# A 23-column key block, raw output weights split inside attention, reordered first loads and a reordered end in a Trainium2 encoder layer

## The chip, the cores and the metric

The kernel runs on one core of one Trainium2 chip. Its engines are TensorE (PE: matmuls, and PEld for the loading of weights), VectorE (DVE), ScalarE (ACT), GpSimd (POOL) and SyncE (SP), whose queue issues nearly all transfers. Each engine takes its instructions in the order of its own queue. The time is that of one execution on the device, in microseconds; the span is the time from the first to the last instruction of the program in a profiled execution.

## The reference

An encoder layer runs over a prompt of 256 tokens and a sample of 2048 tokens, model width 1024, all in float32. After an RMS norm, one projection gives q, k, v, a gate z_a, u_f and a gate z_f, each 512 wide.

```python
q, k, v, z_a, u_f, z_f = jnp.split(proj, ...)
y_a = neighbourhood_attention(q, k, v, rpb)
y_f = fourier_mix(u_f, w_fourier, b_fourier)
mixed = jnp.concatenate([rms_norm(y_a, g_na) * jax.nn.silu(z_a),
                         rms_norm(y_f, g_f) * jax.nn.silu(z_f)], axis=-1)
out = mixed @ w_out
return x + rms_norm(out, g_post)
```

The tokens form a grid of 64 columns. In the neighbourhood attention, each of 8 heads (64 wide) lets a query see 8 rows and 16 columns of keys around it; the columns are worked in four blocks of 16 query columns, each against a slab of up to 32 key columns, with a table of biases added and everything outside the window masked. A query in column c sees key columns from clip(c-8, 0, 48) on, so the queries of the first block (columns 0 to 15) reach key column 22 at most: 23 columns. Fourier mixing is a two-dimensional FFT, a dense layer and a bias.

## The kernel before

Float32 matrices are split into a high and a low part in a reduced-precision type (`F32R`), and a product is made of three matmuls: high-high, high-low, low-high (`mm3`, lines 172 to 175). The stages, in order:

1. The v and u projections for the first row tiles. The first tile's inputs come in pieces (`x_part`, lines 623 to 650): a weight slice `RV`, the vector `gpre`, and x tiles 0, 1, 2. Nine matmuls on ones (`hot`) precede the first real one.
2. The other projections, in two halves of the channels' row groups (lines 749 to 963). Beside the second half, eight blocks of the output weights (128 rows by 1024) are loaded, scaled by `gmix`, split into high and low (`wo_load`, `wo_split`, lines 700 to 710) and stored in `woD`. Blocks 0 to 3 belong to the attention half of `mixed`, blocks 4 to 7 to the Fourier half.
3. The Fourier stage (lines 981 to 1347).
4. The attention stage, a loop over k (lines 1547 to 1635). There are 36 groups `G[k]`: four passes `pr` (two heads each), and in each pass one group for the prompt and eight for the sample, by row group R (0 to 3) and column half hc (0, 1). A group has two column blocks b, whose widths in key columns come from `KW` (line 31). In the loop, iteration k computes the scores of group k (`scores`), adds bias and takes the maximum on DVE (`bias_max`, L1193), exponentiates on ACT (`exps`, L1198), scales by the sum on POOL (`soft`, L1205); and of the group before it transposes the probabilities into the two tiles `ptb` (`transp`, L1469), copies them out (ACT L1471 for the first head, DVE L1473 for the second), and multiplies by V (`pv`, L1486). The PV result is gated on DVE (L1506), squared on ACT (L1512), and the squares are added on POOL (L1513). Between these PE does the Fourier half of the output projection (`f_mm`, L1415), six matmuls after each set of transposes. The order on PE, ACT, DVE, POOL and SP is that of the program text.
5. The attention half of the output projection (lines 1702 to 1733), and for the last tile `last_tile`.

In a group with R>0 a block of w key columns has 11 rows, so 11w keys for each head, in three chunks of 4w, 4w and 3w keys (`prep_v`, lines 1139 to 1142); with R=0 it has 8 rows in two chunks. The rows of the two query halves are laid so that the middle and last chunk hold the same keys for both halves, while the first differs between the halves; so the PV products are two of 128 columns for the shared chunks and two of 64 for the first, for each head.

The attention-half weights are read back from `woD` in iterations 24 to 31 (line 1564) into the two tiles `WO`, which the loop's last iteration (k=36) is the first to use. At the end, `last_tile` (lines 1679 to 1700) works in two column parts, and the residual of the tile before it is done inside it.

Of the kernel before, what the change touches and what calls it, by code (L numbers as in the profile page):

```python
# [18 lines left out]
T = TP + TS  # L19
# [11 lines left out]
KW = (24, 32, 32, 24)  # L31
# [13 lines left out]
def constants():  # L45
# [62 lines left out]
    for p in range(128):  # L108
        half, i, qc = p // 64, p // 16 % 4, p % 16
        for b in range(2):  # L110
            cb = 2 * b + half
            ws = min(max(16 * cb + qc - 8, 0), 48)
            kc = KP0[cb] + np.arange(32)
            cm[p, b] = np.where((kc >= ws) & (kc < ws + 16), 0.0, BIG)
        for cb, j in ((0, slice(0, 24)), (1, slice(24, 56)), (3, slice(56, 80))):
# [62 lines left out]
def build(tc, A, O):  # L178
# [20 lines left out]
    woD = dr.tile([2, 2, 4, 128, D], F32, name="woD")  # L199
# [169 lines left out]
    VC = ((0, 0, 0, 24, 0), (1, 0, 8, 24, 0), (1, 1, 0, 8, 24), (2, 0, 24, 8, 0), (2, 1, 0, 24, 8), (3, 1, 8, 24, 0))  # L369
# [266 lines left out]
    x_part(2, 0)  # L636
# [63 lines left out]
    def wo_load(x):  # L700
        wor[x] = load((128, D), A["wo"][x // 4, x % 4], "wr")

    def wo_split(x):
        w = wor.pop(x)
        g = gmix[:, x:x + 1]
# [3 lines left out]
        for y in range(2):  # L709
            nc.sync.dma_start(woD[x // 4, y, x % 4], f_(o[:, y]))  # L710
# [91 lines left out]
    def at(i, f, *a):  # L802
        hooks.setdefault(i, []).append(call(f, *a))
# [25 lines left out]
    for i in range(16):  # L829
        sg, pr = divmod(i, 8)  # L830
        if i == 8:
# [286 lines left out]
    def prep_v(g):  # L1118
# [99 lines left out]
    for n in range(2):  # L1218
        for c in range(4):
            nc.sync.dma_start(wo1[n][c].bitcast(F32),  # L1220
                              woD[1, :, c, :, n * 512:n * 512 + 512].rearrange("x p d -> p x d"))
# [301 lines left out]

    NT = {4: range(2, 4), 8: range(4, 8), 10: range(8, 13), 12: range(13, 18)}
# [22 lines left out]
    for k in range(2, len(G) + 1):  # L1547
# [11 lines left out]
        if k == 23:  # L1559
# [55 lines left out]
        if f:  # L1615
            pv(f)
        if k == 12:
            pq_.close()
# [40 lines left out]

    def factor(d, q=1):  # L1660
        sa, r = d["sa"], d["r"]
        s, y, x = r[:, 0:1], r[:, 1:2], r[:, 2:3]
        V.tensor_scalar(s, sa[:, q:q + 1], -0.5 / D, sa[:, 4:5], ALU.mult, ALU.add)
# [3 lines left out]
    def residual(d, n):  # L1667
        of, xt, s = d["of"], d["xt"], d["r"][:, 0:1]
        ns = slice(n * 512, n * 512 + 512)
        if "og" in d:  # L1670
            V.scalar_tensor_tensor(out=xt[:, ns], in0=d["og"][:, ns], scalar=s, in1=xt[:, ns], op0=ALU.mult,
                                   op1=ALU.add)
        else:
            V.scalar_tensor_tensor(out=of[:, ns], in0=ptb[n], scalar=s, in1=of[:, ns], op0=ALU.mult, op1=ALU.mult)
            nc.gpsimd.tensor_tensor(out=xt[:, ns], in0=of[:, ns], in1=xt[:, ns], op=ALU.add)
# [3 lines left out]
    def last_tile(d, b):  # L1679
# [12 lines left out]
        residual(b, 1)  # L1692
        sa = d["sa"]
        V.tensor_scalar(sa[:, 0:1], sa[:, 0:1], sa[:, 1:2], None, ALU.add)
# [55 lines left out]
```

## Time and profile before

| What | Value |
|---|---|
| Runs: lowest, median, highest | 959.3, 960.38, 962.52 us |
| The profiled execution | 960.57 us |
| Its span | 958.8 us |
| PE busy | 947.1 us (99%) |
| DVE, ACT, POOL busy | 670.5, 467.9, 332.5 us |
| Moved by DMA | 270.64 MB |
| Granted clock of PE | 0.998 |

In the profile, a row of a timeline gives the start and the length in microseconds, the engine, the line, the operation, what it writes and reads, the shape, and how many instructions were merged; in brackets stand the idle time before it and what ended it. A row of waits gives the total, the count and the longest one. A row of windows gives the stretch, then the busy time of PE, PEld, DVE, ACT and POOL, the granted clock and the share of the DMA engines. A row of one line gives the least, the median and the largest length in nanoseconds. In the timeline a `pv` or `s` product counts as two records.

### The profile page before, as it was taken

Reading aid. Unit: us, or ns where it says so; the run is one execution under the profiler, and the core shown is the slowest. Engines: PE = TensorE matmul, PEld = TensorE weight load, DVE = VectorE, ACT = ScalarE, POOL = GpSimd, SP = SyncE. Lnnn points to the kernel's source line nnn. Section 1 sums busy time; section 2 is a strip of 40 time slices with the busy share of each in tenths; the row PEclk is TensorE's granted clock in tenths of the full one; section 3 lists DMA queues with packets and bytes.
Section 4 is the critical chain, followed back from the end, with each engine's and each line's share of the span. In section 5 each row is a group of like instructions: output and inputs, shape, how many; then the busy total and the mean of one; then the engine's idle time right before and its main releaser. Section 6 shows DMA issues by size and latency. Waiting matters only on the chain.

```text
span 958.8 us, 17851 instructions
## 1 busy us (share of the span) xinstructions
PE 947.1 (99%) x6240; PEld 793.2 (83%) x6240; DVE 670.5 (70%) x1306; ACT 467.9 (49%) x1035; POOL 332.5 (35%) x335
## 2 busy tenths in 40 slices
PE   9999999999999999999999999999999999999996
PEld 7889988888888888888888888888887887888885
DVE  6387987677875975786767454676666555659997
ACT  6845677532333632233444144666565555544443
POOL 3100002445750300533433000454556555424444
PEclk9999999999999999999999999999999999999999
DMA  9899676468665998579979788589898899999993
GB/s 344 315 361 359 216 272 261 166 231 292 241 241 217 363 414 321 208 246 322 332 263 326 282 304 306 211 250 274 277 274 250 253 293 302 267 308 329 335 341 123
DMA packets 158361, 270.64 MB, mean 282 GB/s; under 512 B 22656, under 2 KB 98304, under 8 KB 155392
## 3 DMA queue, kind: packets, MB, share of 16 engines
q1 hardware_dynamic: 157984, 269.37, 81.4%
q8 instruction: 50, 0.82, 0.3%
q14 instruction: 39, 0.32, 0.1%
q10 hardware_dynamic: 288, 0.14, 0.1%
HBM read 180.91 MB, written 95.88 MB: 289 GB/s over the span
## 4 chain that ended last, share of the span: by engine, by line
PE 96%; DVE 1%; DMA 1%; issue 0%; ACT 0%; POOL 0%; DVEq 0%; ACTq 0%; POOLq 0%
PE po L1415 20%; PE mm L174 18%; PE mm L173 18%; PE mm L175 18%; PE pv L1486 5%; PE ptb L1469 5%; PE s L1171 4%; PE pab L1013 2%; PE py L173 1%; PE py L175 1%; PE py L174 1%; DMA yz<-zD 1%; DMA xr<-xt 0%; PE ppq L1051 0%; DMA q<-qD 0%
## 5 line engine op out<-in xcount | busy, mean ns | idle before, releaser
L173 PE MATMUL mm<-xh,wa 128*128 128x512 f32 x448 | 174.4, 389 | 0.0
L174 PE MATMUL mm<-xl,wa 128*128 128x512 f32 x448 | 174.3, 389 | 0.0
L175 PE MATMUL mm<-xh,wa 128*128 128x512 f32 x448 | 174.3, 389 | 0.0
L550 POOL TENSOR_TENSOR ws<-wr 128x512 f32<-128x512 f32 x16 | 21.4, 1336 | 262.4 <-DMA wr<-wz 256.4
L1205 POOL TENSOR_SCALAR w<-w,m 128x352 f32<-128x352 f32 (+4 forms) x136 | 76.9, 578 | 63.2 <-DVE m L1202 53.7
L175 PEld LDWEIGHTS mm<-xh,wa 128*128 128x128 f32 x448 | 84.1, 188 | 17.5
L173 PEld LDWEIGHTS mm<-xh,wa 128*128 128x128 f32 x448 | 84.1, 188 | 17.5
L174 PEld LDWEIGHTS mm<-xl,wa 128*128 128x128 f32 x448 | 84.1, 188 | 17.3
L1415 PE MATMUL po<-wo,yh 128*128 128x512 f32 x272 | 90.5, 413 | 0.0
L1415 PE MATMUL po<-w,yh 128*128 128x512 f32 x280 | 86.7, 391 | 0.0
L565 DVE TENSOR_TENSOR wa<-wr,wa 128x512 fp32r<-128x512 f32 x60 | 56.4, 946 | 30.9 <-ACT wa L564 30.8
L1198 ACT ACTIVATE w<-w,m 128x352 f32<-128x352 f32 (+4 forms) x136 | 70.3, 519 | 13.1 <-DVE m L1193 12.8
L867 DVE TENSOR_TENSOR f<-u,mm 128x512 f32<-128x512 f32 x64 | 43.5, 680 | 33.5 <-PE mm L175 28.7
L174 PE MATMUL mm<-vl,xh 128*128 128x512 f32 x168 | 65.5, 390 | 0.2 <-DVE vl L496 0.2
L175 PE MATMUL mm<-vh,xl 128*128 128x512 f32 x168 | 65.4, 389 | 0.0
L173 PE MATMUL mm<-vh,xh 128*128 128x512 f32 x168 | 65.4, 389 | 0.0
L1415 PEld LDWEIGHTS po<-w,yh 128*128 128x128 f32 x280 | 52.3, 188 | 10.7
L1193 DVE CUSTOM_DVE_ANT_1 w<-s,tb 128x264 f32<-128x264 f32 (+3 forms) x124 | 51.6, 453 | 11.1 <-PE s L1171 10.6
L564 ACT CAST wa<-wr 128x512 fp32r<-128x512 f32 x60 | 36.3, 617 | 41.5 <-PE mm L175 21.4
L1486 PEld LDWEIGHTS pv<-pt,v 96*64 96x64 f32 (+2 forms) x1088 | 45.0, 137 | 13.6 <-issue 9.6
L1415 PE MATMUL po<-w,yl 128*128 128x512 f32 x140 | 54.5, 389 | 0.0
L1415 PE MATMUL po<-wo,yl 128*128 128x512 f32 x136 | 53.5, 393 | 0.0
(244 smaller groups left out, 2204.9 us busy)
## 6 DMA issues: line engine op xcount, KB each, us to landing
wr<-wz SPq DMA_DIRECT2D x48, 512.0 KB
vl<-sD SPq DMA_DIRECT2D x20, 512.0 KB
xm<-xm SPq DMA_DIRECT2D x9, 1024.0 KB
oD<-ofs SPq DMA_DIRECT2D x18, 512.0 KB
of<-oD SPq DMA_DIRECT2D x18, 512.0 KB
yr<-yD SPq DMA_DIRECT2D x34, 256.0 KB
zD<-f SPq DMA_DIRECT2D x16, 512.0 KB
woD<-wo SPq DMA_DIRECT2D x16, 512.0 KB
```

The lines of the kernel that those rows point to most:

```text
L173: nc.tensor.matmul(out, lh, rh, start=first, stop=False)
L174: nc.tensor.matmul(out, lh, rl, start=False, stop=False)
L175: nc.tensor.matmul(out, ll, rh, start=False, stop=last)
L565: nc.vector.tensor_tensor(out=o[:, 1], in0=src, in1=o[:, 0].bitcast(F32), op=ALU.subtract)
L867: nc.vector.tensor_tensor(out=dst(f, b), in0=src(uu[u]), in1=src(p), op=op)
L1171: nc.tensor.matmul(sp[2 * b + h][64 * y:64 * y + 64, j * w:(j + n) * w], g["q"][hs, 128 * b + 64 * y:128 * b + 64 * y + 64], kk[hs, k:k + ...
L1193: nc.vector.tensor_tensor_reduce(out=rows(g["w"][b][:, h, :n], w), in0=rows(g["s"][2 * b + h][:, :n], w), in1=tv, scale=1.0, scalar=3.0e38 ...
L1198: nc.scalar.activation(w, w, AF.Exp, bias=m[:, h:h + 1], scale=-1.0, accum_out=m[:, 2 + h:3 + h])
L1205: nc.gpsimd.tensor_scalar(w, w, m[:, 4 + h:5 + h], 1.0, ALU.mult, ALU.mult)
L1415: nc.tensor.matmul(p, (d["l"] if x == 2 else d["h"])[:, c], w(n, int(x == 1), c), start=j == 0, stop=j == 11)
L1469: nc.tensor.transpose(ptb[h][:nk, j * 128:j * 128 + 128], g["w"][b][:, h, c0:c0 + nk], ident)
L1486: nc.tensor.matmul(p[hs, b, o], g["v"][:nk, v, hs], g["pt"][b][:nk, h, j * 128 + o.start:j * 128 + o.stop], start=first, stop=last)
```

## The change

The diff has four parts.

- The first column block has 23 key columns instead of 24 (`KW`, the masks, the copy of v). Where 11w is at most 256, `prep_v` makes two chunks, of 128 and 11w-128 keys, and loads V in three transfers instead of two.
- `wo_load` and `wo_split` treat the Fourier half only. The attention half is loaded raw within the attention loop, in eight pieces of 128 by 512 (odd k from 13 to 27) into a tile that takes a free slot, and each is split by one ACT and one DVE operation after `pv` in the even iterations from 18 to 32.
- The first requests: `gpre` and x tile 0 go to SP's queue, x tile 2 is the one request on ACT's queue.
- In `last_tile`, the sums come ahead of the residual of the tile before, one small operation comes ahead of a large one, and the last step is shared: 384 and 384 columns on DVE, 256 on ACT and POOL, in three transfers.

```diff
-KW = (24, 32, 32, 24)
+KW = (23, 32, 32, 24)
...
+    nc.sync.dma_start(gpre, A["gpre"])
+    x_part(2, 0, nc.scalar)
     nc.sync.dma_start(RV[0][:, 0], A["wv"][0][:, 0])
-    nc.scalar.dma_start(gpre, A["gpre"])
-    x_part(0, 0, nc.scalar)
+    x_part(0, 0)
...
     nc.sync.dma_start(RV[0][:, 1], A["wv"][0][:, 1])
     x_part(1, 0)
-    x_part(2, 0)
...
-            for x in range(8):
+            for x in range(4):
                 if x:
-                    at(3 * x - 2, wo_load, x)
-                at(3 * x + 2, wo_split, x)
+                    at(6 * x - 2, wo_load, x)
+                at(6 * x + 2, wo_split, x)
...
+            if g["R"] and 11 * w <= 256:
+                vs = src.rearrange("r c e -> (r c) e")[:, cs]
+                k0, k1, m = (r0 - 4) * w, (r1 + 3) * w, 11 * w - 128
+                nc.sync.dma_start(v[:, 4 * b:4 * b + 2], vs[k0:k0 + 256].rearrange("(j p) e -> p j e", p=128))
+                nc.sync.dma_start(v[:n, 4 * b + 2], vs[k1:k1 + n])
+                nc.sync.dma_start(v[n:, 4 * b + 2], vs[k0 + n:k0 + 128])
+                g["ch"].append([(0, 128), (128, m)])
+                g["pp"].append([(1, None, m, 4 * b + 1, True, False), (0, 0, 128, 4 * b, False, False),
+                                (0, 1, 128, 4 * b + 2, False, True)])
+                continue
...
+    def wo_split_a(y):
+        c, ns = wo_part(y)
+        h, l, w = WO[0][:, c, ns], WO[1][:, c, ns], wraw[:, y % 4 * 512:y % 4 * 512 + 512]
+        nc.scalar.activation(h, w, AF.Copy, scale=gmix[:, c:c + 1])
+        V.scalar_tensor_tensor(out=l, in0=w, scalar=gmix[:, c:c + 1], in1=h.bitcast(F32), op0=ALU.mult,
+                               op1=ALU.subtract)
...
-        if 24 <= k < 32:
-            y = k - 24
-            nc.sync.dma_start(WO[y % 2][:, y // 2].bitcast(F32), woD[0, y % 2, y // 2])
+        if 13 <= k < 29 and k % 2:
+            y = (k - 13) // 2
+            c, ns = wo_part(y)
+            nc.sync.dma_start(wraw[:, y % 4 * 512:y % 4 * 512 + 512], A["wo"][0, c][:, ns])
...
         if f:
             pv(f)
+        if 18 <= k < 34 and k % 2 == 0:
+            wo_split_a((k - 18) // 2)
...
-        residual(b, 1)
         sa = d["sa"]
         V.tensor_scalar(sa[:, 0:1], sa[:, 0:1], sa[:, 1:2], None, ALU.add)
         part_sum(sa)
+        residual(b, 1)
         guess(d, 3)
+        half_mean(d, 3)
         V.tensor_tensor(out=og[:, 512:], in0=ptb[1], in1=d["of"][:, 512:], op=ALU.mult)
         factor(d, 3)
-        for n in range(2):
-            residual(d, n)
+        xt, f = d["xt"], d["r"][:, 0:1]
+        nc.scalar.activation(og[:, 768:], og[:, 768:], AF.Copy, scale=f)
+        nc.gpsimd.tensor_tensor(out=xt[:, 768:], in0=og[:, 768:], in1=xt[:, 768:], op=ALU.add)
+        for q, ns in ((nc.sync, slice(0, 384)), (nc.sync, slice(384, 768)), (nc.scalar, slice(768, 1024))):
+            if ns.stop < D:
+                V.scalar_tensor_tensor(out=xt[:, ns], in0=og[:, ns], scalar=f, in1=xt[:, ns], op0=ALU.mult, op1=ALU.add)
+            q.dma_start(O["yo"][d["t"] * 128:d["t"] * 128 + 128, ns], xt[:, ns])
```

More of the change, by code (lines that the diff above doesn't have):

```diff
@@ L114, in constants @@
             cm[p, b] = np.where((kc >= ws) & (kc < ws + 16), 0.0, BIG)
-        for cb, j in ((0, slice(0, 24)), (1, slice(24, 56)), (3, slice(56, 80))):
+        for cb, j in ((0, slice(0, 23)), (1, slice(24, 56)), (3, slice(56, 80))):
             ws = min(max(16 * cb + qc - 8, 0), 48)
@@ L198, in build @@
     yD = dr.tile([2, 4, 128, T], F32, name="yD")
-    woD = dr.tile([2, 2, 4, 128, D], F32, name="woD")
+    woD = dr.tile([2, 4, 128, D], F32, name="woD")
     tD = dr.tile([4, 128, 2, 1520], F32, name="tD")
@@ L1522, in build, with wo_part @@
     WO = []
+    def wo_part(y):
+        return y // 2, slice(y % 2 * 512, y % 2 * 512 + 512)
+    def wo_split_a(y):
[4 more added lines that the diff above has]
+                               op1=ALU.subtract)
     NT = {4: range(2, 4), 8: range(4, 8), 10: range(8, 13), 12: range(13, 18)}
@@ L1669, in residual @@
         ns = slice(n * 512, n * 512 + 512)
[L1670 to L1675, printed above, removed]
+        V.scalar_tensor_tensor(out=of[:, ns], in0=ptb[n], scalar=s, in1=of[:, ns], op0=ALU.mult, op1=ALU.mult)
+        nc.gpsimd.tensor_tensor(out=xt[:, ns], in0=of[:, ns], in1=xt[:, ns], op=ALU.add)
         nc.sync.dma_start(O["yo"][d["t"] * 128:d["t"] * 128 + 128, ns], xt[:, ns])
```

20 lines of the change are left out of this document (12 added, 8 removed).

## The prediction

> **What bounds the kernel now.** I read the page first, then what TensorE (PE) waited for, then the timeline of the attention stage, the first ten microseconds and the last ten.
>
> ```profile
> span 958.8 us, 17851 instructions
> PE 947.1 (99%) x6240; PEld 793.2 (83%) x6240; DVE 670.5 (70%) x1306; ACT 467.9 (49%) x1035; POOL 332.5 (35%) x335
> ...
> PE 96%; DVE 1%; DMA 1%; issue 0%; ACT 0%; POOL 0%; DVEq 0%; ACTq 0%; POOLq 0%
> ```
>
> ```profile
> PE s L1171 <- DMA q<-qD: 0.9, 2, 0.5
> PE pv L1486 <- DMA v<-vD: 0.2, 1, 0.2
> ```
>
> ```profile
> 740.00:780.00 40.00, 40.00 (x477) 32.65 (x474) 23.90 (x85) 23.41 (x73) 21.91 (x35) 1.00 0.91 265
> ```
>
> PE is busy 947.1 of 958.8 us, and 96% of the chain is PE: the program is one long PE queue, idle for 11.7 us in all. In the attention stretch of the last row PE is busy 40.00 of 40.00 us, VectorE (DVE) 23.90, ScalarE (ACT) 23.41. So matmuls taken out of the queue pay in full, and work added to another engine costs nothing until it makes PE's next instruction late. The profiled execution took 960.57 us, 1.8 outside its span; the median of the runs is 960.38, 0.2 less.
>
> **23 columns.** The first column block belongs to groups with hc=0: one in each of four row groups R, in each of four passes pr. In the 12 with R>0, a head's keys shrink from 11x24=264 to 11x23=253, below 256, so three transposed chunks become two. Per group two transposes and two 128-column PV products (one per head) go; the two halves' 64-column products stay.
>
> ```profile
> 708.35 0.86 PE L1469 MATMUL ptb<-ident,w 128*96 128x128 f32 x6
> 746.12 0.66 PE L1469 MATMUL ptb<-ident,w 128*128 128x128 f32 x4
> 712.57 1.57 PE L1486 MATMUL pv<-pt,v 96*64 96x128 f32 x32
> 743.83 1.15 PE L1486 MATMUL pv<-pt,v 96*64 96x64 f32 x32
> 785.64 0.67 PE L1171 MATMUL s<-kk,q 64*64 64x128 f32 x16
> 791.97 0.99 PE L1171 MATMUL s<-kk,q 64*64 64x192 f32 x16
> ```
>
> Six transposes take 0.86, four 0.66: 0.2 for two, up to 0.22 with other pairs of rows. Two PV blocks of 32 records (16 products, two records each) differ only in that half of the products have 128 instead of 64 columns: 0.42 for 8 products, so 64 columns cost 0.0525; a 64-column product is 1.15/16=0.072, a 128-column one 0.125; two are 0.25. Score blocks of 128+128 and 192+256 columns differ by 0.32 over 192 columns, 1.7 ns a column: 11 fewer are 0.02. That is 12 x (0.21+0.25+0.02)=5.8, and about 0.1 for the four R=0 groups: **5.9 us off PE**. That chunks are now 128 keys deep costs nothing: the x6 row with 96-key weights is no shorter than those with 128. One more transfer per group for V lands at worst as late as the one wait on V above, 0.2 x 12=2.4; I take 0, since PE waited for V once in the whole stage, and that in the crowded stretch treated below.
>
> **The attention-half weights.** Before, eight 128x1024 blocks were split while the second half of the channels was projected; four of these splits, their four loads and eight stores go. No row of PE's waits names them, so taking them away gains 0; nor can it lose. In the attention stage eight stored blocks of 512 KB no longer come back; eight raw halves of 256 KB come earlier, in k=13 to 27, and at the end of each even k from 18 to 32 a split is queued: one ACT operation, then a DVE subtraction that needs its result. It stands right behind the PV evacuation, ahead of the next group's bias and maximum (DVE) and exponentials (ACT). Behind these wait the copies out of ptb (L1471, L1473), and the next pair of transposes writes into ptb. The eighth place, and the first:
>
> ```profile
> L263 ACT ACTIVATE wc<-rv,gpre x8: 717/722/726, 4.4 to 13.8; 128x512 fp32r<-128x512 f32 x8
> L264 DVE SCALAR_TENSOR_TENSOR wc<-rv,gpre,wc x8: 743/748/754, 5.8 to 14.6; 128x512 fp32r<-128x512 f32 x8
> ```
>
> ```profile
> 826.18 0.42 DVE L1506 TENSOR_TENSOR y<-pv,za 128x256 f32<-128x256 f32 x1 [0.76 <-PE pv L1486]
> 826.70 0.39 ACT L1512 ACTIVATE sqa<-pv 128x256 f32<-128x256 f32 x1 [3.25 <-DVE y L1506]
> 827.08 0.52 DVE L1193 CUSTOM_DVE_ANT_1 w<-s,tb 128x352 f32<-128x352 f32 x1 [0.47 <-PE s L1171]
> 827.64 0.59 ACT L1198 ACTIVATE w<-w,m 128x352 f32<-128x352 f32 x1 [0.55 <-DVE m L1193]
> 828.23 0.46 ACT L1471 COPY pt<-ptb 96x384 f32<-96x384 f32 x1
> 828.32 0.55 DVE L1473 COPY pt<-ptb 96x384 f32<-96x384 f32 x1
> 829.35 0.81 PE L1469 MATMUL ptb<-ident,w 128*128 128x128 f32 x6
> ```
>
> ```profile
> 734.87 0.38 ACT L1512 ACTIVATE sqa<-pv 128x256 f32<-128x256 f32 x1 [3.20 <-DVE y L1506]
> 734.89 0.36 DVE L1193 CUSTOM_DVE_ANT_1 w<-s,tb 128x192 f32<-128x192 f32 x1
> 735.81 0.24 ACT L1471 COPY pt<-ptb 128x128 f32<-128x128 f32 x1
> 736.82 0.38 PE L1469 MATMUL ptb<-ident,w 128*128 128x128 f32 x2
> ```
>
> The two operations of this shape exist: 0.72 on ACT, 0.75 on DVE. At the eighth place ACT ends its square at 827.09; the split runs to 827.84; DVE begins the subtraction at 827.88 and is free for the bias about 0.67 after that (its operations follow one another a little sooner than they end), at 828.55, not 827.08: 1.47 late. Exponentials and the ACT copy are in line, so the copy ends at 828.69+1.47=830.16, where PE wants to write at 829.35: **0.8 us of PE stall**. At the first place the bias is 1.8 late, the copy ends at 737.87, the transposes wanted to begin at 736.82: 1.1. All eight by the same working: 1.1, 0.8, 0.7, 0.7, 1.0, 1.2, 0.3, 0.8; the seventh is small only because the scores there start late for the query wait shown above; without it, 0.9. Sum **7.2 us**. DVE and ACT catch up before that group's own PV, which begins 0.7 us or more after the second copy, so I count no second stall. The cover would be the 0.6 to 1.0 us between copy and transposes; it is used up, and the rest shows. The bounds: 0, if something lets the subtraction overtake, and 7.2 plus a slower subtraction (a rival below). I take 7.2, because all operations in the line have rows here.
>
> **Lighter traffic.** The waits on queries (0.9) and V (0.2) lie between 801 and 811, where the stored weights came in beside the other loads. Those loads are gone: I take **-0.9**, bounds -1.1 and 0.
>
> **The start.** The first operands are gpre, a weight slice and x0. The change puts gpre and x0 on SP, x0 ahead of the second weight slice, and gives ACT's queue one transfer, x2.
>
> ```profile
> 1.18 0.42 SPq L634 DMA_DIRECT2D rv<-wv  x1
> 4.43 0.72 ACT L263 ACTIVATE wc<-rv,gpre 128x512 fp32r<-128x512 f32 x1 [1.29 <-DMA gpre<-gpre]
> 5.61 0.29 DVE L294 CAST xh<-xr 128x256 fp32r<-128x256 f32 x1 [4.72 <-DMA xr<-xt]
> 6.05 0.77 PE L173 MATMUL mm<-wc,xh 128*128 128x512 f32 x1 [0.85 <-DVE xh L294]
> 8.92 0.63 PE L173 MATMUL mm<-wc,xh 128*128 128x512 f32 x1
> 9.35 0.56 PE L174 MATMUL mm<-wc,xh 128*128 128x512 f32 x1
> 9.75 0.40 PE L175 MATMUL mm<-wc,xl 128*128 128x512 f32 x1
> 9.98 0.39 PE L173 MATMUL mm<-wc,xh 128*128 128x512 f32 x1
> ```
>
> x0 is the last to arrive (cast 5.61); the weight's high part is ready at 5.15. With the weight slice issued one place later (0.4, the length of an issue) that moves to about 5.5, so the first matmul can come 0.5 earlier. At first matmuls start every 0.43 us, from 9.75 every 0.23; if that change of pace stays where it is, 0.5 us of slow pace is worth 0.27 at the later one. I take **-0.3**, bounds 0.4 (the later slice decides) and -0.5. By the Trainium skill, "TensorE: Matmul & The Clock Gate", section "What's actually happening", the clock opens after a busy window of about 3.4 us; the trace fits in that the pace changes 3.3 us after the first matmul. If the shorter gap behind the warm-up matmuls opened it a window sooner, about 1.6 us would go by that page; no row shows it.
>
> **The end.**
>
> ```profile
> 951.68 0.74 DVE L1674 SCALAR_TENSOR_TENSOR of<-ptb,sr,of 128x512 f32<-128x512 f32 x1
> 952.34 0.20 DVE L1694 TENSOR_SCALAR sa<-sa 128x1 f32<-128x1 f32 x1
> 954.36 1.42 DVE L1671 SCALAR_TENSOR_TENSOR xt<-og,sr,xt 128x512 f32<-128x512 f32 x2
> ```
>
> Between 951.68 and the last pair at 954.36 the chain is DVE's own small operations and two long ones, and the change reorders them without removing any; only gaps between small dependent operations close, about 0.2. The last 1.42 becomes two pieces of 384 columns (1.07) beside 256 columns on ACT and POOL, so the last transfer may leave 0.3 sooner; but tile 16's second half leaves later and stands ahead of it. I take **-0.2**, bounds 0.3 and -0.7.
>
> **Sum.** 960.57 - 5.9 + 7.2 - 0.9 - 0.3 - 0.2 = 960.5; less the 0.2 to the median, **960.3 us**.
>
> **The rivals.**
> *The cover holds.* The split fits into DVE's and ACT's idle 40%, PE never waits: 960.3-7.2=953.1. For it: both engines idle 16 us of every 40. Against it: the idle lies at the end of a group, the split in the densest part behind in-order queues. Half the stall is 956.7.
> *The subtraction collides with POOL (slower).* The same operation later in the first stage:
>
> ```profile
> L264 DVE SCALAR_TENSOR_TENSOR wc<-ru,gpre,wc x8: 747/1294/1750, 19.0 to 29.8; 128x512 fp32r<-128x512 f32 x8
> 827.17 0.74 POOL L1513 TENSOR_TENSOR ysq<-ysq,sqa 128x256 f32<-128x256 f32 x1 [1.98 <-ACT sqa L1512]
> ```
>
> Its median is 1.294 instead of 0.748 where POOL also worked. At each split POOL adds the squares (here 827.17 to 827.91), and my subtraction begins at 827.88, just clear. If it collides, each stall grows by up to 0.55: 960.3+4.4=964.7. It decides as soon as the subtraction begins inside POOL's add. By the Trainium skill, "SBUF — State Buffer", section "SBUF: two separate sides", a DVE operation with two SBUF inputs and a reading POOL operation lock each other out for a whole instruction; by that rule a few hundredths of overlap cost hundredths only, and the sum stands.
> *The narrow block does not pay* (V arrives late with its third transfer, 2.4): 962.7, inside the forecast's range.
>
> **How the numbers follow.** Forecast 0.56 (own range 957.8 to 963.0), cover holds wholly or by half 0.26, collision 0.13, late V 0.05. 0.3%, 2.9 us, is about what a measurement of this kernel tells from no change: faster needs less than 957.5, slower more than 963.3. Faster: the cover's 0.26 and 0.05 of the forecast's lower tail, 0.31. Slower: 0.12 of the collision, 0.02 of late V, 0.05 of the forecast's upper tail, 0.19. The same: 0.50. The range reaches from the full cover, nearly, to the collision: 953.6 to 964.6.
>
> **What would show it.** The changed profile should have x4 transposes and shorter PV blocks in 12 groups; new waits of PE (ptb transposes) on ACT's copy, eight times 0.7 to 1.2 us, where there is none now; ACT and DVE rows of 0.72 and 0.75 us directly behind L1512's successor; no PE wait on queries near 800. If PE's busy time falls by 6 and its idle time does not rise, the stall step is wrong; if idle rises by over 10, the collision is right.

## The result and the profile after

The changed kernel takes **966.89 us** (median of 7 runs, 964.71 to 968.96), the kernel before 960.38 (7 runs): ratio 1.0063, 95% interval 1.0047 to 1.0080. That is slower by 6 us, where I forecast 960.3 and a range to 964.6. The profiled execution took 968.96 us; it is the slowest of the seven.

The head of the page of the changed kernel:

```profile
span 967.2 us, 17700 instructions
...
PE 944.5 (98%) x6168; PEld 787.9 (81%) x6168; DVE 673.1 (70%) x1310; ACT 467.5 (48%) x1040; POOL 334.4 (35%) x336
...
PE 88%; DMA 7%; DVE 2%; issue 1%; ACT 1%; SPq 1%; POOL 0%; POOLq 0%; DVEq 0%; ACTq 0%
```

PE has 72 matmuls fewer and is busy 2.6 us less, so the narrower block is there (by the ends of the groups, below, it takes off 4.9). But the span is 8.4 us longer, and PE's share of the chain falls from 96% to 88%, with DMA now at 7%. What PE waits for, by total, count and longest:

```profile
PE pv L1496 <- DMA v<-vD: 5.5, 5, 2.1
PE ptb L1479 <- ACT pt L1481: 5.1, 7, 1.1
...
PE mm L173 <- ACT wc L263: 0.6, 1, 0.6
PE s L1181 <- DMA q<-qD: 0.6, 2, 0.4
PE mm L174 <- DVE wc L264: 0.3, 1, 0.3
```

Three things are new: V late (0.2 before), the transposes behind ACT's copy (none before), and a late weight at the start (none before). I set the ends of the PV products side by side, group by group, in the two traces: a group with R>0 and hc=0 on which no new wait falls is 0.31 to 0.42 us shorter (in the run of this part alone, below, about 0.41 for each of the 12, 4.9 in all); at seven of the eight places with a split PE waits for ACT's copy, up to 1.1 each; five groups wait for V. The attention stage, from the first score to the last PV, takes 7.0 us more.

The timeline of the changed kernel at a split (start, length, then the instruction; in brackets the idle time before it and what ended it):

```profile
778.41 0.38 ACT L1522 ACTIVATE sqa<-pv 128x256 f32<-128x256 f32 x1 [2.67 <-DVE y L1516]
778.69 0.71 ACT L1540 ACTIVATE w<-wraw,gmix 128x512 fp32r<-128x512 f32 x1
...
778.87 0.73 POOL L1523 TENSOR_TENSOR ysq<-ysq,sqa 128x256 f32<-128x256 f32 x1 [1.92 <-ACT sqa L1522]
...
779.43 0.75 DVE L1541 SCALAR_TENSOR_TENSOR w<-wraw,gmix,w 128x512 fp32r<-128x512 f32 x1 [1.12 <-ACT w L1540]
...
780.10 0.42 DVE L1203 CUSTOM_DVE_ANT_1 w<-s,tb 128x253 f32<-128x253 f32 x1
...
780.56 0.51 ACT L1208 ACTIVATE w<-w,m 128x253 f32<-128x253 f32 x1 [1.16 <-DVE m L1203]
...
781.07 0.46 ACT L1481 COPY pt<-ptb 128x384 f32<-128x384 f32 x1
...
781.67 0.83 PE L1479 MATMUL ptb<-ident,w 128*96 128x128 f32 x6 [0.45 <-ACT pt L1481]
```

The line of dependence is the one the prediction drew: the bias stands behind the subtraction, the exponential behind the bias, the copy behind the exponential, and the next transposes behind the copy. The split's two operations take 0.71 and 0.75. The subtraction begins inside POOL's add here (779.43, the add runs from 778.87 to 779.60), and so it does at all eight places; it takes 0.75 at seven of them and 0.86 at the eighth. So POOL does not stretch it by the 0.55 of the rival.

V is the other half. The chain that ended last names these transfers in the changed kernel (start, microseconds from issue to landing). The first four end a wait of PE for V; the last ends a wait in SyncE's queue:

```profile
652.31 8.55 DMA v<-vD
714.25 6.46 DMA v<-vD
...
762.05 7.57 DMA v<-vD
777.13 7.88 DMA v<-vD
790.39 6.00 DMA v<-vD
```

In the program V of a group is requested at the end of the iteration ahead of its own scores. SyncE's queue reaches that request later: the V asked for at 652.31 belongs to a group whose scores began at 647.60, and PE wanted it at 659.59. In the five late groups 5.6 to 7.9 us lie between the first request for V and the moment when PE wants it; a transfer of 6 to 8.5 us has little or no room in that.

How near V comes can be read from the trace for every group, waited for or not: the time from the landing of its last piece to the moment when PE wants the first. Over 31 groups this margin is 3.3 us in the mean in the kernel before and 1.7 in the changed one; it is less than 1 us in 6 of them before and in 14 after.

At the start:

```profile
4.67 0.72 ACT L263 ACTIVATE wc<-rv,gpre 128x512 fp32r<-128x512 f32 x1 [2.01 <-DMA rv<-wv]
...
5.58 0.29 DVE L294 CAST xh<-xr 128x256 fp32r<-128x256 f32 x1 [4.68 <-DMA xr<-xt]
...
7.25 0.72 ACT L263 ACTIVATE wc<-rv,gpre 128x512 fp32r<-128x512 f32 x1 [1.86 <-DMA rv<-wv]
...
8.02 0.51 PE L173 MATMUL mm<-wc,xh 128*128 128x512 f32 x1 [0.59 <-ACT wc L263]
...
11.53 0.52 PE L174 MATMUL mm<-wc,xh 128*128 128x512 f32 x1
11.88 0.40 PE L175 MATMUL mm<-wc,xl 128*128 128x512 f32 x1
```

x0 is cast at 5.58, before at 5.61: asking for it earlier gained nothing. The second weight slice, asked for later, is scaled at 7.25, and PE waits 0.59 for it. The full pace comes at about 11.7 us instead of 9.7. It is a matter of the granted clock; the changed kernel, then the kernel before:

```profile
4.95:8.37 3.42, 1.85 (x6) 0.75 (x4) 1.66 (x4) 1.56 (x4) 0.00 (x0) 1.00 0.96 341
8.37:11.78 3.41, 3.13 (x8) 2.42 (x8) 3.19 (x8) 2.95 (x7) 0.00 (x0) 0.50 0.99 369
```

```profile
9.70:11.78 2.08, 2.08 (x10) 1.69 (x9) 2.05 (x6) 1.87 (x5) 0.00 (x0) 1.00 1.02 383
```

The changed kernel had the full clock from 4.95 on, earlier than the kernel before (from 9.70), and lost it again from 8.37 to 11.78, behind a stretch in which PE was busy for only 1.85 of 3.42 us.

### The profile page after: what moved, and what is told of

Its sections match the earlier page's. It is cut to its first block, busy times and chain, and to the rows that moved or that the text cites. A ratio compares the mean times of both kernels' runs of the same rounds, so it can differ in the third digit from the quotient of the medians.

```text
span 967.2 us, 17700 instructions
## 1 busy us (share of the span) xinstructions
PE 944.5 (98%) x6168; PEld 787.9 (81%) x6168; DVE 673.1 (70%) x1310; ACT 467.5 (48%) x1040; POOL 334.4 (35%) x336
## 4 chain that ended last, share of the span: by engine, by line
PE 88%; DMA 7%; DVE 2%; issue 1%; ACT 1%; SPq 1%; POOL 0%; POOLq 0%; DVEq 0%; ACTq 0%
PE mm L174 18%; PE mm L175 18%; PE mm L173 18%; PE po L1425 17%; DMA v<-vD 4%; PE pv L1496 4%; PE ptb L1479 3%; PE s L1181 3%; PE pab L1013 2%; DMA oD<-ofs 1%; PE py L173 1%; PE py L175 1%; PE py L174 1%; DMA yz<-zD 1%; DMA q<-qD 1%
## 5 line engine op out<-in xcount | busy, mean ns | idle before, releaser
L1215 POOL TENSOR_SCALAR w<-w,m 128x352 f32<-128x352 f32 (+6 forms) x136 | 76.3, 575 | 67.1 <-DVE m L1212 49.2
L565 DVE TENSOR_TENSOR wa<-wr,wa 128x512 fp32r<-128x512 f32 x60 | 60.4, 1014 | 28.3 <-ACT wa L564 28.1
L1208 ACT ACTIVATE w<-w,m 128x352 f32<-128x352 f32 (+6 forms) x136 | 70.0, 518 | 19.7 <-DVE m L1203 19.2
L1496 PEld LDWEIGHTS pv<-pt,v 128*64 128x64 f32 (+4 forms) x1040 | 42.6, 137 | 18.8 <-issue 15.3
L1203 DVE CUSTOM_DVE_ANT_1 w<-s,tb 128x352 f32<-128x352 f32 (+5 forms) x124 | 51.3, 451 | 8.3 <-PE s L1181 8.0
L1479 PE MATMUL ptb<-ident,w 128*128 128x128 f32 (+3 forms) x332 | 49.6, 280 | 5.2 <-ACT pt L1481 5.1
```

Source lines behind the costliest of these rows:

```text
L565: nc.vector.tensor_tensor(out=o[:, 1], in0=src, in1=o[:, 0].bitcast(F32), op=ALU.subtract)
L1203: nc.vector.tensor_tensor_reduce(out=rows(g["w"][b][:, h, :n], w), in0=rows(g["s"][2 * b + h][:, :n], w), in1=tv, scale=1.0, scalar=3.0e38 ...
L1208: nc.scalar.activation(w, w, AF.Exp, bias=m[:, h:h + 1], scale=-1.0, accum_out=m[:, 2 + h:3 + h])
L1215: nc.gpsimd.tensor_scalar(w, w, m[:, 4 + h:5 + h], 1.0, ALU.mult, ALU.mult)
L1479: nc.tensor.transpose(ptb[h][:nk, j * 128:j * 128 + 128], g["w"][b][:, h, c0:c0 + nk], ident)
L1496: nc.tensor.matmul(p[hs, b, o], g["v"][:nk, v, hs], g["pt"][b][:nk, h, j * 128 + o.start:j * 128 + o.stop], start=first, stop=last)
```

## The experiments

The runs of "before" differ a little from one set of runs to the next (medians 959.95 to 961.23), so each ratio is against those of its own set. In the diffs `...` stands for lines left out.

**The four parts alone.**

```diff
 narrow_block_alone: KW, masks, VC and prep_v of the change, nothing else
-KW = (24, 32, 32, 24)
+KW = (23, 32, 32, 24)
...
 raw_weights_alone: wo_load, wo_split, woD, wraw, wo_split_a
+        if 18 <= k < 34 and k % 2 == 0:
+            wo_split_a((k - 18) // 2)
...
 first_requests_alone:
+    nc.sync.dma_start(gpre, A["gpre"])
+    x_part(2, 0, nc.scalar)
...
 end_chain_alone: half_mean, residual, last_tile
```

> The kernel before with the 23-column block alone. Theory A (the narrow transfers of V, 92 rows landing over only 4 of the DMA engines, make V late): PE's queue is 4.9 us shorter (0.41 for each of 12 groups), but PE waits on V for 3 to 6 us, so the time is -2 to +1 us against before, and the V transfers' landings come as 12 early and 4 late. Theory B (V is late only because the weights' split delays the queues): no V waits, 4.9 us faster.

> The kernel before with the raw attention-half weights and their split in the attention loop alone. My stall theory: PE waits eight times for the copy out of ptb, 0.6 to 1.2 us each, about 6.5 in all, less the query waits of before (0.9): +5 to +6.5 us. The rival (the split is covered, and the stalls came only with the late V): within 1 us of before.

> The kernel before with the reordered first requests alone. Theory C (the second weight slice, two places later on SP's queue, comes late, and the faster pace of the matmuls starts later with it): +1 to +1.5 us, and the stages behind start that much later. Rival (one slow transfer in the profiled execution was chance): within 0.5 us of before, or 0.3 faster.

> The shorter end chain alone. The forecast's step: 0.2 us less, bounds +0.3 and -0.7. From the changed kernel's profile, where PE's end to the end of the span takes 7.33 instead of 7.42 us: 0.1 less. Either is the same time within what can be measured: 960 to 962 us, ratio 0.999 to 1.001; the profile shows the stretch behind PE's last instruction.

| Part | Median, us | Ratio, 95% interval | By the ratio |
|---|---|---|---|
| 23 columns | 962.94 | 1.0020 [1.0006, 1.0034] | +1.9 us |
| raw weights | 964.37 | 1.0041 [1.0025, 1.0056] | +3.9 |
| first requests | 961.72 | 1.0007 [0.9994, 1.0021] | +0.7 |
| end chain | 960.45 | 0.9996 [0.9984, 1.0008] | -0.4 |

The parts multiply to 1.0064; the whole is 1.0063. With intervals of 0.12% to 0.16% to either side of each part that does not exclude that they act on one another, but each part can be looked at by itself. The 23 columns, the part with the sure gain, make the kernel slower. Each group of 12 is 0.41 shorter in its trace, 4.9 us, so some 6.8 us go lost elsewhere. PE's waits in that run, for V and for the queries:

```profile
PE pv L1496 <- DMA v<-vD: 1.9, 2, 1.3
...
PE s L1181 <- DMA q<-qD: 0.4, 1, 0.4
```

They are 2.3 us, but this profiled execution was the fastest of 12 (958.54); the median is 4.4 longer. So one profile's waits don't price this part. Behind the waits it shows a second cost, the clock:

```profile
799.74 0.45 PE L1496 MATMUL pv<-pt,v 92*64 92x64 f32 x8 [1.30 <-DMA v<-vD]
800.78 1.28 PE L1496 MATMUL pv<-pt,v 92*64 92x64 f32 x24 [0.59 <-DMA v<-vD]
```

```profile
802.29:805.71 3.42, 3.21 (x29) 2.59 (x30) 1.63 (x7) 1.18 (x4) 0.72 (x1) 0.50 1.04 325
```

Two waits of together 1.9 us are followed by 3.4 us at half the clock; PE was busy for 1.68 of the 3.41 us before. What the slower executions wait for no profile shows.

In the run of the raw weights V and the queries are on time, and in the attention stage PE waits for nothing but the copies:

```profile
PE ptb L1469 <- ACT pt L1471: 5.5, 8, 1.1
```

Eight times, 5.5 us.

**Is it the splits' place?** The same part, with the split queued ahead of `f_evac` instead of behind `pv`:

```diff
+        if 18 <= k < 34 and k % 2 == 0:
+            wo_split_a((k - 18) // 2)
         if k == 34:
             ys_split(atiles[0])
...
         if f:
             pv(f)
-        if 18 <= k < 34 and k % 2 == 0:
-            wo_split_a((k - 18) // 2)
```

> The kernel before with the raw weights alone, each split moved up in the same even iteration to where the odd iterations split the Fourier tiles, ahead of the evacuation of the projection and of PV. Stall theory: the copies out of ptb are on time again, the eight PE waits (5.5 us) are gone, the lighter traffic stays: 0 to 1.5 us faster than before. Rival (the split costs wherever it stands): +2 us or more.

959.56 us, ratio 0.9994 [0.9975, 1.0013], against 1.0041 with the split behind `pv`. The waits on the copies are gone. Waits on V and on queries are back, though the traffic is that of the run above:

```profile
PE pv L1486 <- DMA v<-vD: 1.0, 2, 0.7
...
PE s L1171 <- DMA q<-qD: 0.6, 2, 0.4
```

So the same two operations cost 4.5 us in one place and nothing that can be measured in the other: the stall mechanism of the prediction is shown. And the lighter traffic alone does not bring V and the queries in time: in the run above, it seems, the stalls gave them that time.

**Why is V late? Width, or number of requests.** The change's V comes in pieces of 92 and 36 rows. Of 92 rows only five completions are counted in the trace, of 36 rows thirteen, of 128 rows sixteen. By the Trainium skill, "DMA: Bandwidth & Descriptors", section "Why a DMA increments its semaphore by 16 and not by 1", a transfer runs on the largest number of engines, up to 16, that divides its number of rows. The trace agrees: that is 4 and 12, and one count more, which comes 0.5 us after the request and well ahead of the others. The suspicion was that few engines are slow.

```diff
 narrow_block_cut_transfers: 92 -> 80 + 12 rows, 36 -> 32 + 4 rows, at R=0 also (not shown)
-                nc.sync.dma_start(v[:n, 4 * b + 2], vs[k1:k1 + n])
-                nc.sync.dma_start(v[n:, 4 * b + 2], vs[k0 + n:k0 + 128])
+                for p0, p1, k in ((0, 80, k1), (80, 92, k1), (92, 124, k0), (124, 128, k0)):
+                    nc.sync.dma_start(v[p0:p1, 4 * b + 2], vs[k + p0:k + p1])
 one_more_request: kernel before, the 96-row piece of V in the 12 groups cut 48 + 48
+                if g["R"] and w == 24 and b == 0 and m == 1:
+                    for p0, p1 in ((0, 48), (48, n)):
+                        nc.sync.dma_start(v[p0:p1, 4 * b + j], rows_[p0:p1])
 one_more_request_narrow: the same, cut 92 + 4
+                    for p0, p1 in ((0, 92), (92, n)):
...
```

> As the run with the 23-column block alone, but each V transfer of 92 or 36 rows is cut in two, 80 and 12 rows, 32 and 4 rows, so that most rows come in multiples of 16; the bytes are the same, the requests more. Theory A: the V waits of the uncut run go, 4 to 5 us faster than before. Theory B: the same time as the uncut run, or slower by the extra requests.

> The kernel before, 24 columns, with the 96-row transfer of V of the first block (R>0) cut into 48 and 48 rows: 12 requests more, the same bytes, each half over 16 engines. Theory D (SP's transfers take turns on eight semaphores, so each request waits for the landing of the one eight places earlier; one more request takes 4.4/8=0.55 us of a queue that is nearly full, and V comes late): V waits of PE, 1 to 6 us slower than before. Theory A (only narrow transfers hurt): within 1 us of before.

> As the run with 48 and 48 rows, but cut into 92 and 4 rows, each of which lands over 4 engines only. Theory A: slower than the even cut by 2 us or more, and V landings with 4 late engines. Theory D: as the even cut, within 1.5 us.

Cutting the pieces so that they spread evenly, with 32 requests more, gives 973.34 us, 1.0135 [1.0117, 1.0153]:

```profile
PE pv L1496 <- DMA v<-vD: 9.5, 8, 2.7
PE s L1181 <- DMA q<-qD: 2.5, 4, 1.0
```

One more request per group in the kernel *before*, 12 in all, with the same bytes, costs 1.0042 [1.0021, 1.0062] cut evenly and 1.0031 [1.0014, 1.0048] cut 92 and 4. The profile of the even cut shows V late where the last pass begins, with a stretch at half the clock behind it (804.30 to 807.72):

```profile
PE pv L1491 <- DMA v<-vD: 2.6, 1, 2.6
```

Evenly cut is no better, so the width does not show as a cause, though the intervals leave room for some 2 us either way. The landings say the same: between the twelfth and the last of sixteen completions lie 0.83 us in the mean in the narrow block alone and 0.79 in the kernel before, which has no narrow piece. The number of requests is a cause: 3 to 4 us for 12 requests, without any gain or loss in the arithmetic.

**Fewer requests.**

```diff
 narrow_block_one_request: V of the first block is copied into HBM in the order in
 which a group uses it, beside the projections; one request per group
+                nc.sync.dma_start(v[:, :k], vX[g["R"]][:128 * k].rearrange("(j p) e -> p j e", p=128)[:, :, cs])
 narrow_block_za_merged: the two pieces of za (R=0 and R=2) with one request
+            nc.sync.dma_start(g["za"].rearrange("p (b x) -> p b x", b=2),
+                              zD[1, cs].rearrange("p (k x) -> p k x", x=128)[:, i:j + 1:j - i])
 narrow_block_third_on_act: the 36-row piece on ScalarE's queue
-                nc.sync.dma_start(v[n:, 4 * b + 2], vs[k0 + n:k0 + 128])
+                nc.scalar.dma_start(v[n:, 4 * b + 2], vs[k0 + n:k0 + 128])
 narrow_block_za_on_act: za of the 12 groups on ScalarE's queue
-            nc.sync.dma_start(g["za"][:, x:x + n], ...)
+            (nc.scalar if g["R"] and not g["hc"] else nc.sync).dma_start(g["za"][:, x:x + n], ...)
...
```

> The kernel before with the 23-column block alone, but V of that block is laid out in HBM beforehand (four more copies per row group in the projection stage), so that each group loads it in one request of 128 rows: one request less than before instead of one more, and no narrow one. Theories A and D both: PE does not wait on V for that block, 4 to 5.5 us faster than before. If neither the count nor the width is the cause: as the 23-column block alone, 0 to 3 us slower than before.

> The 23-column part alone; in the groups with R=0 and R=2 the two pieces of za come with one request instead of two (16 requests fewer in the stage, so 4 fewer than in the kernel before; same bytes, same packets, all on SyncE's queue). Theory of the number of requests: waits on V mostly under 2 us, 957 to 959.5 us, ratio 0.996 to 0.999. Rival (bytes: the transfer engines are full): as the narrow block alone, 962 to 964, ratio 1.001 to 1.003.

> The 23-column part alone, as in the run of that part alone, but the 36-row piece of V (the one request per group that was added, 12 in all) is issued on ScalarE's queue instead of SyncE's. Same bytes, same pieces, same total of requests; only SyncE's queue with its eight semaphores has the number of requests of the kernel before. Theory (one more request on SyncE's queue makes V late): the waits on V fall back to at most 2 us, the 12 groups keep their 0.41 each, 956.5 to 958.5 us, ratio 0.995 to 0.998. Rival (the pieces themselves, the bytes or the memory make V late, whichever queue asks): V waits stay and so does the time, 962.0 to 964, ratio 1.001 to 1.003.

> The 23-column part alone; V's pieces as in the change, all on SyncE's queue, but in the same 12 groups the gate values za (16 requests, a tile of their own, so ScalarE has nothing to wait for) are issued on ScalarE's queue: SyncE has 4 requests fewer than in the kernel before, bytes and pieces are those of the narrow block. Theory of the queue (one request more on SyncE's eight semaphores makes V late): waits on V under 2 us, 957 to 959 us, ratio 0.996 to 0.998. Rival (V's last rows are late at one group ahead whoever asks, because the transfer engines are behind): as the narrow block alone, 962 to 964, ratio 1.001 to 1.003. ScalarE's issues take 0.3 us each and may cost up to 0.3 in a group where the copies out of ptb are tight: up to 1.5 in all on either side.

One request: 959.79 us, 0.9983 [0.9968, 0.9997]. Merged za (16 requests fewer): 958.97, 0.9983 [0.9970, 0.9997]. Both turn the narrow block's 1.0020 into a small gain, 1.6 us of the 4.9. For the merged za that is what the number of requests foretold; the one request was to bring 4 to 5.5, and in its profile PE still waits 2.6 us, once, for just that V. The profile of the merged one still has V late at one place, where a new pass begins and its tables are loaded too:

```profile
PE pv L1500 <- DMA v<-vD: 3.5, 2, 3.1
```

ScalarE's queue was no cure: 964.67 us, 1.0036 [1.0023, 1.0050], and 965.31, 1.0055 [1.0036, 1.0075]. There ScalarE itself stood still at a request until another transfer had landed, and the exponentials behind it were late; from the first of the two, on ScalarE:

```profile
659.71 0.30 ACTq L1139 DMA_DIRECT2D v<-vD  x1
660.05 0.51 ACT L1208 ACTIVATE w<-w,m 128x253 f32<-128x253 f32 x1 [4.68 <-DMA v<-vD]
```

PE waited 6.4 and 6.1 us for copies out of ptb in these two. Which transfer ScalarE stood still for can be read from the semaphores, the counters on which a transfer reports its landing. SyncE's requests use eight of them in turn, and ScalarE's use the same eight in the same turn: the request at 659.71 goes out 0.14 us after the landing (659.57) of the V transfer that had its semaphore before, and ten of the twelve moved requests go out within 0.25 us of such a landing. (In the second run it is 14 of 16.) The expectations of these two runs assume that a request on ScalarE's queue leaves SyncE's turn. It does not, so they say nothing on whose queue makes V late.

**Fewer bytes, or an earlier request.**

```diff
 narrow_block_half_bytes_out: leaves out half of the Fourier half's output (not stored);
 later the stored half is read back for both, with two requests instead of one
-            nc.sync.dma_start(oD[t * 128:t * 128 + 128, :], o)
+            nc.sync.dma_start(oD[t * 128:t * 128 + 128, :512], o[:, :512])
...
 narrow_block_v_two_ahead, v_two_ahead_alone (kernel before): VB = 4, and
+    prep_v(G[3])
...
-        if k + 1 < len(G):
-            prep_v(G[k + 1])
+        if k + 2 < len(G):
+            prep_v(G[k + 2])
```

> The 23-column part alone; of the first half's output tiles only 512 of 1024 columns are stored to HBM in the attention stage, with the same number of requests (leaves out half of that output; later the stored half is read back for both). About 4 MB fewer of some 60 MB in the stage. Theory of the number of requests: V stays late, 961 to 963.5 us, ratio 1.000 to 1.003. Rival (bytes): waits on V vanish, 956 to 958.5 us, ratio 0.995 to 0.998.

> The 23-column part alone with V and za asked for two groups ahead instead of one (four buffers instead of three). Both theories: no wait on V, the gain of 4.9 us that the 12 groups show stays, 956 to 957 us, ratio 0.995 to 0.996. If it stays above 960, late V is not where the gain went.

> The kernel before with V and za two groups ahead and nothing else: the part that the earlier request has of itself. Its profile shows 0.2 us of waits on V, so 960 to 961 us, ratio 0.999 to 1.000; if its other executions often wait for V, 958 to 960.

With the requests of the narrow block and 4.7 MB fewer (265.81 against 270.53 MB) it takes **955.39 us**, 0.9949 [0.9931, 0.9967]: as much as the whole 4.9 us of the arithmetic. Its six executions lie within 1.5 us (954.82 to 956.32), the twelve of the narrow block within 7.6. What fewer bytes would bring the kernel before was not run; its profile has 1.1 us of waits on V and queries to lose. The waits, and then the stretch from 620 to 850 us in this kernel, in the narrow block alone and in the kernel before (busy time of PE, PEld, DVE, ACT, POOL; granted clock, share of the DMA engines, GB/s):

```profile
PE s L1181 <- DMA q<-qD: 1.1, 2, 0.6
...
PE pv L1497 <- DMA v<-vD: 1.0, 2, 0.6
```

```profile
620.00:850.00 230.00, 227.94 (x2598) 185.43 (x2598) 141.23 (x520) 136.87 (x435) 119.94 (x184) 1.00 0.87 256
```

```profile
620.00:850.00 230.00, 227.61 (x2565) 184.87 (x2564) 141.63 (x519) 137.19 (x435) 120.36 (x184) 0.99 0.91 271
```

```profile
620.00:850.00 230.00, 228.77 (x2619) 186.81 (x2614) 142.51 (x514) 137.23 (x432) 120.19 (x184) 1.00 0.91 270
```

The engines that move data are busy 0.91 of that stretch in the kernel before, the highest share beside PE's. With 0.87 V's margin is 3.0 us in the mean again (2.5 in the narrow block alone), and below 1 us in 3 groups of 31 instead of 6. My expectation from the number of requests alone, 961 to 963.5, fell; the rival's came in (955.39 is just below its 956 to 958.5), though V's waits did not vanish: 1.0 us is left. And the number of requests counts too, as the runs above show. I read this as one margin that both use up.

The expectation for V two groups ahead fell as well: 967.30 us, 1.0073 [1.0055, 1.0092] with the narrow block, 966.66, 1.0068 [1.0054, 1.0082] in the kernel before. V is never late there; the queries are. In the kernel before with V two ahead:

```profile
PE s L1171 <- DMA q<-qD: 5.6, 4, 3.6
```

```profile
807.70 2.33 PE L1171 MATMUL s<-kk,q 64*64 64x264 f32 x24 [3.59 <-DMA q<-qD]
...
816.36 1.28 PE L1171 MATMUL s<-kk,q 64*64 64x352 f32 x24
```

```profile
807.60:816.30 8.70, 8.60 (x76) 6.79 (x76) 3.51 (x13) 3.00 (x10) 3.32 (x5) 0.68 1.00 284
816.30:825.00 8.70, 8.70 (x115) 7.14 (x110) 5.50 (x20) 5.34 (x15) 3.88 (x6) 1.00 0.88 256
```

Putting one load forward only moves the lateness to the next. And a wait of 3.59 us costs more than itself: a narrower block of scores behind it takes 2.33 us where a wider one takes 1.28 later, at a granted clock of 0.68 instead of 1.00, and that group is 5.3 us longer than in the kernel before. By the Trainium skill, "TensorE: Matmul & The Clock Gate", section "What's actually happening", the clock falls back to half after an idle window of about 3.4 us. The trace agrees for this wait, but a window need not be idle throughout here: in the narrow block alone waits of 1.30 and 0.59 us, with PE busy for 1.68 of 3.41 us, were enough.

**Whole versions.** All parts but the first requests, with the early split, and V by one of the ways above.

```diff
 all_but_start_third_on_act, all_but_start_one_request (R=0 keeps chunks of 92 rows),
 all_but_start_v_two_ahead: edits as above, together
```

> The whole change without the reordered first requests, with the 36-row piece of V on ScalarE's queue and each weight split queued ahead of f_evac instead of behind the PV evacuation. If the parts add up (23 columns with the request off SyncE -4, raw weights with the early split -1.6, end -0.1): 955 to 957 us, ratio about 0.995. If the raw loads and the other requests still make V late together: 959 to 962. If the stall mechanism is not what the early split took away, 961 to 964.

> As the last, but V of the first column block lies ready in one piece in HBM, for each row group, so that a group asks for it with one request (one fewer than in the kernel before; about ten more requests in the projections, where the pieces are copied). In the groups with R=0 it keeps chunks of 92 rows. Theory of the queue: 955 to 957 us, ratio 0.994 to 0.996, waits on V under 2 us. If the copies in the projections delay the work there as they seemed to with this layout alone: about 957 to 959.

> The whole change without the reordered first requests, each weight split queued ahead of f_evac, V two groups ahead. If late V and the stalls behind the splits are all that stood against the change: 23 columns -4.9, weights -1 to -1.6, end -0.1, so 954 to 956 us, ratio 0.993 to 0.995. If something else eats the gain: 958 or more.

963.41 us (1.0034 [1.0016, 1.0052]), 959.80 (0.9988 [0.9970, 1.0006]) and 965.82 (1.0060 [1.0039, 1.0080]). The second runs from 955.78 (the profiled one) to 965.77. All three expectations of 954 to 957 us fell. The first result lies where a wrong stall mechanism was expected (961 to 964), but in its profile PE waits for late copies four times, up to 3.3 us, and not eight: they are again ScalarE's own waits at requests. None of the three is clearly better than the narrow block with merged za, which beats both kernels, by 0.17% the one before.

## Why the prediction was wrong

**The step that failed** is the sentence on V's third transfer: "lands at worst as late as the one wait on V above, 0.2 x 12=2.4; I take 0, since PE waited for V once in the whole stage". That PE had hardly waited says nothing of how near it was. A sign of it stood in a row that I had read, the DMA share of 0.91 in the first row of windows; I read that row for PE, DVE and ACT only. The margin itself is in the trace of the kernel before: V lands 3.3 us ahead of its use in the mean, but less than 1 us ahead in 6 groups of 31. The runs show +1.9 us for this part where I had -5.9: the arithmetic gives 4.9, so 6.8 are lost. That transfers make up this loss follows from the run with fewer bytes, in which it is gone; the one profile of this part, its fastest execution, shows 2.3 us of waits and 3.4 us at half the clock behind them. The bound of 2.4 was too small by almost three times, because I scaled a wait that happened to be seen instead of asking what the transfer takes (6 to 8.5 us in the late cases) against the time it has (5.6 to 7.9 us), and put nothing down for the clock. The rival that named the mechanism, "the narrow block does not pay", had 0.05 and this same 2.4.

**The 23 columns on PE**: 5.9 forecast, 4.9 found (12 groups of 0.41). The transposes gave 0.19 as said; PV gave 0.22, not 0.25; the R=0 groups almost nothing. Mechanism right, size a little off. As much as 4.9 shows in time only when bytes are taken out.

**The eight stalls**: 7.2 forecast, 5.5 found in the run of the weights alone, eight times, up to 1.1. The mechanism is right, down to the instruction that is late; the early split confirms it. The rival "the cover holds" falls. So does the collision with POOL: its condition is met at all eight places (the subtraction begins inside POOL's add, not just behind it as I had worked out), and still it takes 0.75, once 0.86. The sign that I gave for it, PE's idle time up by over 10 us, came all the same (from 11.7 to 22.7): from waits on V and on copies that are late without a collision. It was no sign of the collision alone.

**Lighter traffic**: -0.9. In the weights alone no wait on V or queries is left, as forecast: 5.5-1.1=4.4 by the waits, 3.9 by the ratio. But with the split moved, and the same traffic, PE waits 1.0 for V and 0.6 for queries; before it was 0.2 and 0.9. So the gain is not shown to be the traffic's: the stalls hid the lateness. In the whole change, with the narrow block's requests, V's waits are back (5.5 us in its slowest execution).

**The start**: -0.3 with a bound of +0.4; the runs say +0.7 with an interval of -0.6 to +2.0. Whether it loses time at all is not shown. The step was wrong in its cause: x0 does not land sooner when it is asked for sooner, and the second weight slice, which I let come 0.4 later, stands two places later in SyncE's queue and is scaled 1.84 later (at 7.25; in the timeline of the kernel before ACT begins with it at 5.41). I also took the clock's opening as fixed. By the clock's records in the traces the full clock comes at 9.70 in the kernel before, 3.65 us after the first real matmul (the pace changes with the matmul at 9.75, not at 3.3 us), but of the 18 kernels here with the start as before ten have it at 4.1 to 5.6 us and eight at 9.4 to 10.5. One of the ten loses it again for 3.41 us; of the two with the reordered start both have it early and both lose it (8.37 to 11.78 and 8.77 to 12.19). So the opening a window sooner, which I named, did come here, and was lost again. How much is lost also varies without any change: the first step behind the first row tiles begins at 51.47 us in the kernel before, at 50.33 in the run of the end alone, at 52.60 in that of the first requests.

**The end**: -0.2; from PE's last matmul to the end it takes 7.32 us instead of 7.42 in the run of the end alone, and the ratio is 0.9996. That agrees, though so small a gain cannot be told from no change.

The sum by the runs: +1.9+3.9+0.7-0.4=6.1 us, against my -0.1. Of the 6.2 between them, 7.8 lie in the 23 columns and 1.0 in the start; the weights, whose +6.3 came out as 3.9, take 2.4 off, the end 0.2. The chance of 0.19 for slower was put on stalls and POOL, too little on transfers.

**What stays open**: how much of a request's cost comes from requests waiting for one another, and how much from what each costs the engines that carry it out. That they wait for one another is shown. In the trace of the kernel before SyncE's transfers use eight semaphores strictly in turn (37 or 38 requests on each between 640 and 850 us), and never more than eight are on their way, 6.3 in the mean; a request waits until the one eight places earlier has landed, and 68 of the 299 go out within 0.25 us of that landing. SyncE's own waits show such waits without any shared data, here a query request behind a store of output tiles:

```profile
SPq L1115 <- DMA oD<-ofs: 4.8, 8, 0.9
```

With 4.44 us from issue to landing in the mean, one more request takes about 4.44/8=0.55 us of that queue, an estimate from these two numbers. That fits the direction of the runs with more and with fewer requests, but the two runs that were to show it on another queue could not, since ScalarE's requests take their turn on the same eight semaphores, and fewer bytes made up the loss with every request in place.

## What to carry to other kernels

A stage in which PE is busy all the time and the engines for transfers are busy 0.9 has two bounds. Price each new request and each moved byte as well as each removed matmul, and read the margin of a load (time from request to use against time to land), not whether it was waited for in one execution. Work for idle engines belongs where their queues are empty, not where their share is low: the same split cost 4.5 us behind `pv` and nothing that could be measured ahead of `f_evac`.

## What the hardware showed that I had not expected

- Twelve requests more, same bytes, cost 0.31% to 0.42% of the whole kernel (3 to 4 us).
- A transfer's completions come unevenly: that of V issued at 652.31 us has twelve of its sixteen by 5.9 us and the last at 8.55. Pieces of 92 rows show five completions instead of sixteen, and yet no difference in time could be measured between a piece cut 48+48 and 92+4.
- Waits of PE cost more than themselves, and short ones can too: a wait of 3.59 us is followed by 8.7 us at a mean granted clock of 0.68, two waits of 1.30 and 0.59 us by 3.4 us at 0.50; a wait of 2.68 us (in the run with cut transfers, at 722.19) is followed by no loss of clock.
- In this program the requests of SyncE and ScalarE take turns on the same eight semaphores, so a request moved to ScalarE's queue makes ScalarE wait for a transfer of SyncE's.
- Executions of one kernel spread by some 7 us on one chip: the narrow block alone from 958.54 to 966.14 us (12 runs), the kernel before beside the last parts from 958.21 to 965.30 (35 runs). One profile shows one of them.
